# Hybrid diffusion layer on one core: twelve dense blocks beside the state scan instead of eight, merge-gate blocks ahead of attention

## The chip, the cores and the metric

The kernel runs on one core of a Trainium2 chip. The core has five engines with a queue each: TensorE (PE in the profile, with weight loads as PEld), VectorE (DVE), ScalarE (ACT), GpSimd (POOL) and SyncE (SP), which issues the DMAs here. An engine takes its instructions in the order of its queue; semaphores make it wait for others. The metric is the device time of one execution in microseconds.

## What is computed

Two layers (DEPTH = 2) over 128 context and 1024 latent tokens, 1152 together, D_MODEL = 1024, three branches 512 wide. Cut to what matters:

```python
def mixer_layer(x, cvec, lw, ctx_kv, ssm_h0, rope):
    ...
    h = rmsnorm(x, norm_g) * (1.0 + scale) + shift
    a_in, a_gate, f_in, f_gate, q, k, v, c_gate = jnp.split(h @ w_in, SPLITS, axis=-1)
    ya, finals = s5_mixer(a_in, ...)          # state scan, forward and backward
    za = jax.nn.gelu(ya) @ glu_w
    ya = za[..., :BRANCH_W] * jax.nn.sigmoid(za[..., BRANCH_W:])
    yf = fourier_mix(f_in) @ fnet_w
    ...
    yc = blocked_attention(q, k, v)           # 8 heads, 2 key heads, over 1152 keys
    branches = jnp.stack([ya * jax.nn.silu(a_gate), yf * jax.nn.silu(f_gate),
                          yc * jax.nn.silu(c_gate)], axis=2)
    proj = jnp.einsum('bsnw,nwd->bsnd', branches, w_branch)
    g = jax.nn.sigmoid(h @ merge_w + merge_b).reshape(b, s, N_BRANCH, D_MODEL)
    merged = jnp.sum(g * proj, axis=2)
    return x + gate * (merged @ w_out), k, v, finals
```

## The kernel before

Every large product is cut into dense blocks: 128 output columns, three token tiles j of 384, and K in pieces of 128 (eight for products of h, four for those of a branch). A float32 operand is split into a high and a low part; each K piece takes three matmuls (high by high, high by low, low by high) of 128x384 into a PSUM tile pd (two buffers). `dense` (line 269) yields after every four K pieces, so a **unit** is 12 matmuls; a block of K = 1024 has six units, one of K = 512 three. For every 512 rows of weights, SP loads wst, ACT copies the high part to whi and POOL subtracts to get wlo; loads run three units ahead, splits one. After its last matmul a tile is evacuated: store blocks by ACT (Silu or copy) to a tile jo (three buffers) and to DRAM, gate blocks by ACT (tanh), proj blocks by DVE (jo<-th,pd or jo<-jt,pd, then for the second and third branch jo<-jo,jt with the partial sum).

`layer` (line 1290) puts all blocks of a layer in one list and takes them from it by number. `drive` merges generators: each has a rate, and the one whose virtual time is least goes next. What it emits is then ordered for each engine by the scheduler of the language, which places an instruction when its own estimate of times lets it start; so an instruction can stand elsewhere in an engine's queue than in the program. Stages of layer 0, in order:

- a_in and f_in blocks, with set-up of the state space, then `state_gen`, which makes the inputs of the scan.
- **Scan**: `scan_gen` (line 706): 128 steps of four dependent DVE instructions on H (A in the profile), 128x128 for the first 16 steps, 128x64 after them. At step 24 it calls `finals` (line 728): ACT copies the state of step 16 to ss_fin, PE transposes it, ACT copies it out (qk_sq), SP stores it. Beside it run eight dense blocks (a and f gates). The q, k, v generator has started and has split its weights (qkW).
- **q, k, v**: per 128 tokens 24 matmuls into a PSUM tile pt (two buffers); ACT sums squares (qk_j), DVE and POOL make qk_ss and qk_rs, DVE reads pt into qk_xn. Two dense blocks beside it.
- **Output of the scan** (`ssm_out_gen`) with six blocks, **GLU** with nine, **Fourier** (`fnet_gen`) with three.
- **Attention** (`attn_gen`): 64 steps, a head and 128 queries each. A step is: six matmuls into pa (scores, one buffer), DVE's maximum at_mx, ACT's exponential at_P, DVE's reciprocal and scaling of at_P; then the nine transposes of the step before, split by ACT and DVE into at_PT; every second step 18 matmuls P·V into pv, ACT at_t, DVE at_Y. `PACE` says how many units of dense work follow an even and an odd step: (1, 2).
- zc load, gates and projections of the third branch, output product, then the same for layer 1.

In attention, `merges` takes the dense list: one gate block, the four Fourier output blocks, one gate block beside the split load of branch a (`zload_gen`: tiles jt and jo, ACT A<-jt and A<-jo, POOL the rest), eight proj blocks, one gate block beside the load of branch b, then gates and projections of branch b in turn.

Of the kernel before, what the change touches and what calls it, by code (L numbers as in the profile page):

```python
# [17 lines left out]
D = 1024  # L18
# [3 lines left out]
NT = SP + SL  # L22
# [62 lines left out]

PACE = (1, 2)
HELD = 2
# [14 lines left out]
class Program:  # L102
# [71 lines left out]

    # ---------------------------------------------------------------- constants
    def setup(self):
# [57 lines left out]

    # ---------------------------------------------------------------- weights
    def wload(self, ap):
# [56 lines left out]

    # ---------------------------------------------------------------- adaLN
    def ada_alloc(self, l):
# [91 lines left out]

    # ---------------------------------------------------------------- token-major x to feature-major
    def load_x(self, t0, t1):
# [27 lines left out]

    # ---------------------------------------------------------------- norm
    def ssq_alloc(self):
# [105 lines left out]

    # ---------------------------------------------------------------- S5
    def ssm_setup_gen(self, l):
# [178 lines left out]
    def scan_gen(self, l):  # L706
        S, H = self.S, self.H
        for k in range(128):
            n = 2 if k < 16 else 1
            if n == 2:  # L710
                cur, nxt = H[:, :, :, k:k + 18:17], H[:, :, :, k + 1:k + 19:17]
                AR = S["AR"][:, :, :, None].to_broadcast([128, 2, 32, 2])
                AI = S["AI"][:, :, :, None].to_broadcast([128, 2, 32, 2])
            else:
                cur, nxt = H[:, :, :, k + 17:k + 18], H[:, :, :, k + 18:k + 19]
                AR, AI = S["AR"][:, :, :, None], S["AI"][:, :, :, None]
            t1 = self.sb("ss_s1", [128, 2, 32, 2], bufs=2, pool=self.gp)
            t2 = self.sb("ss_s2", [128, 2, 32, 2], bufs=2, pool=self.gp)
            t1, t2 = t1[:, :, :, :n], t2[:, :, :, :n]
            self.tt(t1, AR, cur, OP.mult)  # L720
            self.tt(t2, AI, cur[:, ::-1], OP.mult)
            self.tt(t1, t1, nxt, OP.add)
            self.tt(nxt, t1, t2, OP.add)
            if k == 24:
                self.finals(l)
            yield 800

    def finals(self, l):
# [89 lines left out]

    # ---------------------------------------------------------------- q, k, v
    def qkv_tables(self, l):  # L820
# [168 lines left out]

    # ---------------------------------------------------------------- FNet  # L990
    def fnet_tables(self):
# [81 lines left out]

    # ---------------------------------------------------------------- attention
    def softmax(self, src, n, P):
# [159 lines left out]

    # ---------------------------------------------------------------- the layers
    def zload_gen(self, z_d, zf, dve=True, held=0):
# [52 lines left out]
    def layer(self, l, cs):  # L1290
# [15 lines left out]
        zt = {}  # L1306
# [49 lines left out]
        def proj_block(n, b, th, key):  # L1356
            def ev(j, ps):
                t = self.jt(rows(th["d"], b, j)) if "d" in th else th.pop(j)
                pt = self.jt(rows(t_d[n - 1], b, j)) if n > 0 else None
# [12 lines left out]
        tha = {"d": dt_("tha", (D, NT))}  # L1372
        thb = {"d": dt_("thb", (256, NT))}

# [36 lines left out]
        self.dense_add(self.store_blocks(w_in, C_CG, 4, sg_d[2], AF.Silu))  # L1411
        self.dense_add([gate_block(0, b, tha) for b in range(5)])
        self.dense_add(glu_blocks())
        self.dense_add([gate_block(0, b, tha) for b in range(5, 8)])
        self.dense_add([gate_block(1, 0, thb)])
        self.dense_add(fw_blocks())
        self.dense_add([gate_block(1, 1, thb)])
        self.dense_add([proj_block(0, b, tha, "a") for b in range(8)])
        for b in range(2, 8):
            th = {}  # L1420
            self.dense_add([gate_block(1, b, th), proj_block(1, b, th, "b")])
            if b < 4:
                self.dense_add([proj_block(1, b - 2, thb, "b")])
        self.dense_add([gate_block(2, b, thc[b]) for b in range(8)])
# [5 lines left out]
        with self.spool:  # L1430
# [11 lines left out]
            with self.pool("qp", l):  # L1442
                with self.pool("gp", l, "q"):
                    self.qkt = self.qkv_tables(l)
                    def qkv():
                        yield from self.qkv_gen(l, qs_d, k_d, v_d, (0,))
                        yield from self.qkv_gen(l, qs_d, k_d, v_d, (1,))
                    q = qkv()
                    self.run_some(q, 8)
                    drive((self.scan_gen(l), 103), (self.dense(8), 106))  # L1450
                    drive((q, 78), (self.dense(2), 21))
# [6 lines left out]
        with self.pool("gp", l, "f"):  # L1458
            self.fnet_tables()
            zt["f"] = self.sb("A1", [128, 2, 4, NT], R)  # L1460
            run(self.dense(1))
            drive((self.dense(2), 32), (self.fnet_gen(l, f_d, zt["f"]), 48))
        with self.pool("gp", l, "a"):
            def merges():
# [5 lines left out]
                yield from self.beside(self.zload_gen(zb_d, zt["b"], False, 2), self.dense(1), 1)  # L1470
                yield from self.dense(13)
            m = merges()
# [122 lines left out]
```

## Time and profile before

| what | value |
|---|---|
| device time of three runs | 2791.06, 2797.77, 2800.18 us; median 2797.77 |
| span of the profiled execution, first to last instruction | 2790.2 us |
| median of the runs less that span | 7.6 us |
| busy: PE, DVE, ACT, POOL | 94%, 65%, 42%, 24% |
| mean granted TensorE clock | 0.975 of 2.4 GHz |

The device time of the profiled execution itself is not listed apart from its span. Stages of layer 0 by the timeline: scan 190 to 353 us, q, k, v to 462, output of the scan to 518, GLU to 645, Fourier to 735, attention to 1158. Times on the timeline are microseconds from the start of the span; in brackets stands the time that the engine sat idle before an instruction, and what ended it.

### The profile page before, as it was taken

To read this page: it belongs to the slowest core of one execution; us is meant where nothing else is said; L and a number is where in the kernel's file an instruction comes from. 1 tells how busy PE (TensorE), PEld (TensorE's weight loads), DVE (VectorE), ACT (ScalarE), POOL (GpSimd) and SP (SyncE) were. 2 spreads that over 40 slices of the span, in tenths; PEclk is the share of its full clock that TensorE was granted. 3 is DMA by queue.
4 is the path that set the end of the run, shared out by engine and by line. 5 is a ranking of instruction groups with operands and counts; after the bars stand their busy time and mean duration, and the time that the engine had idled before them with its cause. 6 is when DMAs were issued, how large, how long until landed. Compare 5 with 4: busy or idle time off the path is not lost.

```text
span 2790.2 us, 44375 instructions
## 1 busy us (share of the span) xinstructions
PE 2615.0 (94%) x16092; PEld 2516.5 (90%) x16092; DVE 1807.5 (65%) x3933; ACT 1158.2 (42%) x2688; POOL 679.0 (24%) x521
## 2 busy tenths in 40 slices
PE   7998698999999999999999895989999999999998
PEld 3998698998999999999989895979989999999997
DVE  6559956764577777766573797575666777771343
ACT  5461154432455555423345322543235454553244
POOL 3231123222321210132343220322233020102223
PEclk9999899999999999999999997999999999999999
DMA  6632134474444422444542321356626444213244
GB/s 223 174 101 88 49 111 120 138 213 159 159 144 148 140 87 74 136 125 118 170 143 83 99 92 37 112 147 171 220 96 214 133 125 139 80 47 94 82 121 145
DMA packets 449627, 352.68 MB, mean 126 GB/s; under 512 B 71800, under 2 KB 421632, under 8 KB 449408
## 3 DMA queue, kind: packets, MB, share of 16 engines
q1 hardware_dynamic: 448112, 345.59, 40.5%
q0 software_dynamic: 1296, 4.26, 0.5%
q8 instruction: 127, 2.08, 0.3%
q14 instruction: 92, 0.75, 0.1%
HBM read 236.44 MB, written 113.31 MB: 125 GB/s over the span
## 4 chain that ended last, share of the span: by engine, by line
PE 65%; DVE 20%; issue 5%; DMA 5%; ACT 3%; POOL 1%; SPq 0%; DVEq 0%; POOLq 0%; ACTq 0%
PE pd L168 41%; DVE ss_s L145 7%; PE pa L168 7%; PE pv L168 6%; PE pt L168 6%; PE pt L173 4%; DVE A L145 3%; PE pv L173 2%; DVE xr L149 1%; DMA aw<-in_ada_w_dram 1%; DVE hl L149 1%; DVE jo L149 1%; DMA tha<-jo 1%; DVE jo L145 1%; ACT A L142 1%
## 5 line engine op out<-in xcount | busy, mean ns | idle before, releaser
L168 PE MATMUL pd<-hh,whi 128*128 128x384 f32 x2496 | 859.4, 344 | 25.6 <-ACT jo L142 20.9
L168 PE MATMUL pd<-hh,wlo 128*128 128x384 f32 x2496 | 844.2, 338 | 3.1 <-POOL wlo L145 3.1
L168 PE MATMUL pd<-hl,whi 128*128 128x384 f32 x2496 | 843.1, 338 | 1.4 <-DVE hl L149 1.4
L145 POOL TENSOR_TENSOR wlo<-wst,whi 128x512 fp32r<-128x512 f32 x312 | 436.8, 1402 | 1541.4 <-ACT whi L142 1451.7
L168 PEld LDWEIGHTS pd<-hh,whi 128*128 128x128 f32 x2496 | 472.2, 189 | 36.5 <-ACT jo L142 23.5
L168 PEld LDWEIGHTS pd<-hh,wlo 128*128 128x128 f32 x2496 | 472.5, 189 | 7.7 <-POOL wlo L145 5.8
L168 PEld LDWEIGHTS pd<-hl,whi 128*128 128x128 f32 x2496 | 473.2, 190 | 5.3 <-DVE hl L149 2.3
L168 PE MATMUL pd<-A,whi 128*128 128x384 f32 x1728 | 449.1, 340 | 8.3 <-ACT jo L142 4.5
L168 PEld LDWEIGHTS pd<-A,whi 128*128 128x128 f32 x1728 | 307.5, 189 | 12.3 <-DVE jo L149 6.2
L142 ACT ACTIVATE whi<-wst 128x512 fp32r<-128x512 f32 x312 | 195.8, 630 | 245.8 <-PE pd L168 167.9
L168 PE MATMUL pd<-A,wlo 128*128 128x384 f32 x864 | 290.0, 336 | 0.0
L168 PE MATMUL pt<-qkW,hh 128*128 128x384 f32 x576 | 154.4, 350 | 59.3 <-DVE qk_xn L145 59.3
L1079 DVE TENSOR_REDUCE at_mx<-pa 128x1 f32<-128x1152 f32 x128 | 173.4, 1355 | 54.6 <-PE pa L168 54.2
L142 ACT ACTIVATE at_PT<-pt 128x384 fp32r<-128x384 f32 (+1 forms) x260 | 113.9, 490 | 188.5 <-PE pt L173 188.3
L142 ACT ACTIVATE at_P<-pa,at_mx 128x1152 f32<-128x1152 f32 x128 | 158.3, 1236 | 18.2 <-DVE at_mx L1079 17.7
L168 PEld LDWEIGHTS pd<-A,wlo 128*128 128x128 f32 x864 | 162.8, 188 | 0.1
L168 PEld LDWEIGHTS pt<-qkW,hh 128*128 128x128 f32 x576 | 107.5, 196 | 60.0 <-DVE qk_xn L145 60.0
L168 PE MATMUL pa<-at_K,at_Q 128*128 128x384 f32 x768 | 160.4, 338 | 1.1 <-DMA at_K<-kd 1.0
L168 PE MATMUL pv<-at_PT,at_V 128*128 128x256 f32 x1152 | 149.7, 284 | 0.2
L168 PEld LDWEIGHTS pv<-at_PT,at_V 128*128 128x128 f32 x1152 | 142.7, 190 | 4.6 <-DVE at_PT L145 0.8
L168 PEld LDWEIGHTS pa<-at_K,at_Q 128*128 128x128 f32 x768 | 131.5, 188 | 4.9 <-DMA at_K<-kd 2.1
L145 DVE TENSOR_TENSOR at_PT<-pt,at_PT 128x384 fp32r<-128x384 f32 (+1 forms) x260 | 132.2, 549 | 2.3 <-ACT at_PT L142 2.2
(295 smaller groups left out, 3715.4 us busy)
## 6 DMA issues: line engine op xcount, KB each, us to landing
aw<-in_ada_w_dram SPq DMA_DIRECT2D x48, 512.0 KB, 4.3
wst<-in_merge_w_dram SPq DMA_DIRECT2D x96, 256.0 KB, 3.0
wst<-in_w_in_dram SPq DMA_DIRECT2D x80, 256.0 KB, 2.9
td<-jo SPq DMA_DIRECT2D x96, 192.0 KB, 2.7
jt<-td SPq DMA_DIRECT2D x96, 192.0 KB, 2.7
wst<-in_w_out_dram SPq DMA_DIRECT2D x64, 256.0 KB, 2.7
sgd<-jo SPq DMA_DIRECT2D x72, 192.0 KB, 1.9
jt<-sgd SPq DMA_DIRECT2D x64, 192.0 KB, 3.3
```

What stands on the lines that cost most here:

```text
L142: return self.nc.scalar.activation(out, in_, func, **kw)
L145: return (e or self.nc.vector).tensor_tensor(out=out, in0=a, in1=b, op=op)
L149: return (e or self.nc.vector).scalar_tensor_tensor(out, a, s, b, op0=op0, op1=op1, **kw)
L168: return self.nc.tensor.matmul(out, w, x, start=first, stop=last, **kw)
L173: return self.nc.tensor.transpose(out, in_, i[:n, :n])
L1079: nc.vector.tensor_reduce(out=mx[:, 0:1], in_=src, axis=AX.XY if m3 else AX.X, op=OP.max, negate=True)
```

## The change

The list of blocks is put in another order, and the numbers that the stages take are changed with it: the scan gets twelve blocks (a, f and c gates) in place of eight, q, k, v and the scan's output get gate 0 blocks in place of c gates, GLU starts with a gate 1 block, Fourier gets four gate 1 blocks in place of three gate 0 blocks, and attention three gate 1 blocks in place of eight. `PACE` goes from (1, 2) to (1, 1), so attention's units fall from 108 to 78. All eight gate 1 blocks keep their tanh in DRAM (thb), and the projection loads it back to a tile th; before, two did and six kept it on chip. `finals` is called after the scan's last step.

```diff
-PACE = (1, 2)
+PACE = (1, 1)
...
-            if k == 24:
-                self.finals(l)
             yield 800
+        self.finals(l)
...
         def proj_block(n, b, th, key):
             def ev(j, ps):
-                t = self.jt(rows(th["d"], b, j)) if "d" in th else th.pop(j)
+                if n == 1:
+                    t = th_tile()
+                    self.dma(t, rows(th["d"], b, j))
+                else:
+                    t = self.jt(rows(th["d"], b, j)) if "d" in th else th.pop(j)
...
-        thb = {"d": dt_("thb", (256, NT))}
+        thb = {"d": dt_("thb", (D, NT))}
...
-        self.dense_add([gate_block(0, b, tha) for b in range(5)])
+        self.dense_add([gate_block(0, b, tha) for b in range(8)])
+        self.dense_add([gate_block(1, 0, thb)])
         self.dense_add(glu_blocks())
-        self.dense_add([gate_block(0, b, tha) for b in range(5, 8)])
-        self.dense_add([gate_block(1, 0, thb)])
+        self.dense_add([gate_block(1, b, thb) for b in range(1, 6)])
         self.dense_add(fw_blocks())
-        self.dense_add([gate_block(1, 1, thb)])
+        self.dense_add([gate_block(1, 6, thb)])
         self.dense_add([proj_block(0, b, tha, "a") for b in range(8)])
-        for b in range(2, 8):
...
+        self.dense_add([gate_block(1, 7, thb)])
+        self.dense_add([proj_block(1, b, thb, "b") for b in range(8)])
...
-                    drive((self.scan_gen(l), 103), (self.dense(8), 106))
+                    drive((self.scan_gen(l), 103), (self.dense(12), 140))
...
-            drive((self.dense(2), 32), (self.fnet_gen(l, f_d, zt["f"]), 48))
+            drive((self.dense(3), 48), (self.fnet_gen(l, f_d, zt["f"]), 48))
...
                 yield from self.beside(self.zload_gen(zb_d, zt["b"], False, 2), self.dense(1), 1)
-                yield from self.dense(13)
+                yield from self.dense(8)
```

What it moves in the engines' queues is shown at three places. The first is ACT early in the scan of layer 0, before the change (jo are the evacuations of the dense tiles, ss_fin the copy of the final state, qk_sq its way out):

```order
L142 ACT_TABLE_LOAD
L142 ACTIVATE jo<-pd 128x384 x2
L142 ACTIVATE whi<-wst 128x512
L142 ACTIVATE ss_fin<-A_1197 128x64
L142 ACTIVATE whi<-wst 128x512
L142 ACTIVATE jo<-pd 128x384 x3
L142 ACTIVATE whi<-wst 128x512
L142 ACTIVATE qk_sq<-pv 32x128 x2
```

And ACT at the same place after it:

```order
L142 ACT_TABLE_LOAD
L142 ACTIVATE jo<-pd 128x384 x2
L142 ACTIVATE whi<-wst 128x512
L142 ACTIVATE ss_fin<-A_1197 128x64
L142 ACTIVATE whi<-wst 128x512
L142 ACTIVATE jo<-pd 128x384 x3
L142 ACTIVATE whi<-wst 128x512 x2
```

ss_fin keeps its place behind two jo and a whi; qk_sq has moved to the end of the stage.

The second is POOL through the scan of layer 0, as a piece of the difference (wlo is the low part of a weight tile, qk_rs the scale of the q, k, v rows):

```order
 L145 TENSOR_TENSOR wlo<-wst,whi 128x512 x2
 L145 TENSOR_TENSOR qkW_1994<-jt,qkW_1993 128x384
-L145 TENSOR_TENSOR wlo<-wst,whi 128x512 x16
+L145 TENSOR_TENSOR wlo<-wst,whi 128x512 x24
 L145 TENSOR_TENSOR qk_rs<-qk_ss,half 128x4 x7
 L145 TENSOR_TENSOR wlo<-wst,whi 128x512
```

Eight more weight splits stand ahead of the first qk_rs.

The third is DVE in attention of layer 0, where projections of branch b run beside it. Before the change, one step without P·V and the beginning of the next:

```order
L1079 TENSOR_REDUCE at_mx<-pa 128x1
L145 TENSOR_TENSOR at_PT_10973<-pt,at_PT_10972 128x3x128 x2
L145 TENSOR_TENSOR at_PT_10973<-pv,at_PT_10972 128x3x128
L1082 RECIPROCAL at_mx<-at_mx 128x1
L1083 TENSOR_SCALAR at_P<-at_P,at_mx 128x1152
L149 SCALAR_TENSOR_TENSOR jo<-th,pd 128x384
L145 TENSOR_TENSOR jo<-jo,jt 128x384
L1079 TENSOR_REDUCE at_mx<-pa 128x1
```

After it, such a step and the next:

```order
L1078 TENSOR_REDUCE at_mx<-pa 128x1
L145 TENSOR_TENSOR at_PT_12013<-pt,at_PT_12012 128x3x128 x2
L145 TENSOR_TENSOR at_PT_12013<-pv,at_PT_12012 128x3x128
L1081 RECIPROCAL at_mx<-at_mx 128x1
L149 SCALAR_TENSOR_TENSOR jo<-th,pd 128x384
L1082 TENSOR_SCALAR at_P<-at_P,at_mx 128x1152
L1078 TENSOR_REDUCE at_mx<-pa 128x1
L145 TENSOR_TENSOR at_PT_12013<-pt,at_PT_12012 128x3x128 x2
L145 TENSOR_TENSOR at_PT_12013<-pv,at_PT_12012 128x3x128
L145 TENSOR_TENSOR jo<-jo,jt 128x384
L1081 RECIPROCAL at_mx<-at_mx 128x1
```

The first half of the projection's evacuation, which reads pd, has moved ahead of the scaling of at_P. On PE, the step without P·V has 11 or 12 dense matmuls between its transposes and the next scores, where 24 stood.

## Rows read from the trace of the kernel before

**Rows 1.** Page, part 1: busy us, share and count of each engine.
```profile
PE 2615.0 (94%) x16092; PEld 2516.5 (90%) x16092; DVE 1807.5 (65%) x3933; ACT 1158.2 (42%) x2688; POOL 679.0 (24%) x521
```

**Rows 2.** Waits of PE: who waited for whom; us in total, times, longest.
```profile
PE pt L168 <- DVE qk_xn L145: 59.3, 2, 29.7
PE pd L168 <- ACT jo L142: 25.4, 8, 7.8
```

**Rows 3.** Windows: us, busy PE, PEld, DVE, ACT, POOL (instructions), clock, DMA share, GB/s.
```profile
190.00:353.20 163.20, 124.92 (x704) 123.29 (x702) 153.46 (x539) 30.52 (x68) 30.84 (x22) 0.89 0.24 76
735.00:1158.00 423.00, 422.17 (x2805) 414.41 (x2803) 310.12 (x523) 221.37 (x456) 73.47 (x60) 1.00 0.39 123
```

**Rows 4.** Timeline of PE where the scan ends: start, us, instruction, [idle before].
```profile
310.69 0.52 PE L168 MATMUL pt<-qkW,hh 128*128 128x384 f32 x2
...
323.17 0.34 PE L168 MATMUL pd<-hh,wlo 128*128 128x384 f32 x1
353.17 1.01 PE L168 MATMUL pt<-qkW,hh 128*128 128x384 f32 x2 [29.67 <-DVE qk_xn L145]
...
1711.37 1.01 PE L168 MATMUL pt<-qkW,hh 128*128 128x384 f32 x2 [29.64 <-DVE qk_xn L145]
```

**Rows 5.** Windows around the two stalls of layer 0's scan; the clock is third from the end.
```profile
230.00:310.00 80.00, 80.00 (x464) 79.65 (x463) 75.41 (x268) 17.31 (x34) 16.45 (x13) 1.00 0.27 87
...
353.20:359.10 5.90, 5.90 (x19) 5.90 (x20) 2.41 (x9) 2.31 (x12) 1.01 (x1) 0.50 0.23 69
...
224.90:229.30 4.40, 4.35 (x14) 4.36 (x15) 4.19 (x15) 0.37 (x1) 0.96 (x1) 0.50 0.46 149
```

**Rows 6.** Timeline of DVE at the scan's last instruction.
```profile
351.26 0.28 DVE L145 TENSOR_TENSOR A<-ss_s,ss_s 128x64 f32<-128x64 f32 x1
```

**Rows 7.** Timeline of ACT and PE at ss_fin.
```profile
223.68 0.32 ACT L142 ACTIVATE ss_fin<-A 128x64 f32<-128x64 f32 x1 [12.25 <-DVE A L145]
...
224.95 0.69 PE L168 MATMUL pd<-hh,whi 128*128 128x384 f32 x1 [7.83 <-ACT jo L142]
```

**Rows 8.** Timeline of POOL and DVE in the scan, at a weight split.
```profile
309.39 1.28 POOL L145 TENSOR_TENSOR wlo<-wst,whi 128x512 fp32r<-128x512 f32 x1 [9.12 <-ACT whi L142]
...
309.13 0.28 DVE L145 TENSOR_TENSOR A<-ss_s,ss_s 128x64 f32<-128x64 f32 x1
309.44 1.36 DVE L145 TENSOR_TENSOR ss_s<-ss_AR,A 128x64 f32<-128x64 f32 x1
```

**Rows 9.** Windows of two attention steps each, projections of branch b and a.
```profile
1000.83:1013.35 12.52, 12.52 (x86) 12.36 (x85) 9.42 (x17) 6.51 (x13) 1.30 (x1) 1.00 0.42 135
...
830.29:842.81 12.52, 12.52 (x86) 12.35 (x85) 9.36 (x17) 5.92 (x12) 1.30 (x1) 1.00 0.39 116
```

**Rows 10.** Timeline of PE in an attention step: scores and the first dense matmul.
```profile
1005.80 1.20 PE L168 MATMUL pa<-at_K,at_Q 128*128 128x384 f32 x6
...
1007.75 0.42 PE L168 MATMUL pd<-hh,whi 128*128 128x384 f32 x1
```

**Rows 11.** Timeline of DVE and ACT in the same step.
```profile
1007.04 1.36 DVE L1079 TENSOR_REDUCE at_mx<-pa 128x1 f32<-128x1152 f32 x1 [0.82 <-PE pa L168]
...
1010.05 0.82 DVE L1083 TENSOR_SCALAR at_P<-at_P,at_mx 128x1152 f32<-128x1152 f32 x1
...
1008.50 1.24 ACT L142 ACTIVATE at_P<-pa,at_mx 128x1152 f32<-128x1152 f32 x1
```

**Rows 12.** The tile at_P on DVE: ns min/median/max, first and last start.
```profile
L1083 DVE TENSOR_SCALAR at_P<-at_P,at_mx x128: 809/821/1502, 755.5 to 2510.3; 128x1152 f32<-128x1152 f32 x128
```

**Rows 13.** Timeline of PE where the second key block is loaded.
```profile
955.96 0.80 PE L168 MATMUL pa<-at_K,at_Q 128*128 128x384 f32 x3 [0.15 <-DMA at_K<-kd]
```

**Rows 14.** Timeline of ACT where branch b is loaded and split.
```profile
910.05 0.53 ACT L142 ACTIVATE A<-jo 128x384 fp32r<-128x384 f32 x1 [0.53 <-DMA jo<-zbd]
```

**Rows 15.** A short wait of PE in q, k, v, and the window after it.
```profile
400.00 0.62 PE L173 MATMUL pa<-identr,qk_kk 128*128 128x128 f32 x3 [1.83 <-ACT qk_qo L142]
...
400.00:403.40 3.40, 3.40 (x14) 3.40 (x15) 3.37 (x9) 1.54 (x6) 1.46 (x2) 0.51 0.92 271
```

More of the change, by code (lines that the diff above doesn't have):

```diff
@@ L1411, in layer @@
         self.dense_add(self.store_blocks(w_in, C_CG, 4, sg_d[2], AF.Silu))
-        self.dense_add([gate_block(0, b, tha) for b in range(5)])
+        self.dense_add([gate_block(0, b, tha) for b in range(8)])
+        self.dense_add([gate_block(1, 0, thb)])
         self.dense_add(glu_blocks())
-        self.dense_add([gate_block(0, b, tha) for b in range(5, 8)])
-        self.dense_add([gate_block(1, 0, thb)])
+        self.dense_add([gate_block(1, b, thb) for b in range(1, 6)])
         self.dense_add(fw_blocks())
-        self.dense_add([gate_block(1, 1, thb)])
+        self.dense_add([gate_block(1, 6, thb)])
         self.dense_add([proj_block(0, b, tha, "a") for b in range(8)])
-        for b in range(2, 8):
[L1420 to L1423, printed above, removed]
+        self.dense_add([gate_block(1, 7, thb)])
+        self.dense_add([proj_block(1, b, thb, "b") for b in range(8)])
         self.dense_add([gate_block(2, b, thc[b]) for b in range(8)])
```

## Prediction

> **What bounds the kernel now.** I read the page's busy shares first, then who waited for whom on TensorE (PE), then busy time by stage, then the timeline where PE stood still. PE is busy 94% of the span [rows 1], so a change pays only where it takes away PE idle time, or moves PE work into it. PE's waits have two big entries, both from one place in each of the two layers: 59.3 us in two waits on VectorE's (DVE's) qk_xn and 25.4 us in eight waits on ScalarE's (ACT's) jo [rows 2]. The stage table agrees: in the state-scan stage (190 to 353.2 us) PE works 124.9 of 163.2 us, while in attention (735 to 1158 us) it works 422.2 of 423 us [rows 3]. The reader is to see that before the change attention has no PE time to give away and the scan stage has 38 us of it.
>
> The timeline shows the hole. PE finishes the eight dense blocks, starts the q/k/v product at 310.69 us and stops at 323.5; it resumes at 353.17 after 29.67 us, and in layer 1 at 1711.37 after 29.64 us [rows 4]. What it waits for stands behind the scan in DVE's queue: the scan's last instruction runs at 351.26 us [rows 6]. After the hole PE's clock is at its lower level: from 353.2 to 359.1 the granted clock is 0.50, that is 1.2 GHz, against 1.00 (2.4 GHz) in the run before [rows 5]. That costs half of 5.9 us, 2.95 us more.
>
> **The change part by part.**
>
> *Four more blocks beside the scan.* A dense matmul takes 80.00 us / 464 = 0.1724 us at full clock [rows 5]; a unit (four k, three matmuls each) is 12 of them, 2.07 us. A block of eight k is six units, so four more blocks are 24 units, 288 x 0.1724 = 49.7 us. PE therefore ends the dense blocks at 310.7 + 49.7 = 360.4 us, and has its 12.8 us of q/k/v work (310.7 to 323.5) before it needs qk_xn, at 373.2 us. Does the scan end by then? Each dense unit of this kind brings a weight split on GpSimd (wlo on POOL), and the DVE instruction of the scan that meets it takes 1.36 us in place of 0.28 [rows 8]; sixteen such splits become 24 in the stage (the order of POOL shows x16 against x24). So the scan ends 8 x 1.08 = 8.6 us later, at 351.5 + 8.6 = 360.1 us, and qk_xn follows within 2 us. PE needs it 11 us after that. The hole closes and with it the slow-clock stretch: 29.67 + 2.95 = 32.6 us a layer, **65.2 us** in all. If the cover were gone (a scan 11 us longer than reckoned), each further microsecond would be one of PE's again.
>
> *The final states (finals) after the scan instead of at step 24.* One would expect 7.83 us a layer here: at 223.68 us ACT takes up ss_fin after 12.25 us of waiting for the scan's step 16, jo behind it frees no PSUM, and PE stands 7.83 us and then runs 4.4 us at half clock [rows 5, 7]. But the order shows ss_fin at the same place of ACT's queue as before, behind the same two jo and one whi, because the instruction depends only on that step and the scheduler places it by its own estimate. So the stall stays; I cost the edit at **0**. Behind ss_fin wait, as before, whi and three jo, and PE for these. What does move is the transpose of ss_fin on PE and its copy, to the end of the stage, where two small matmuls cost nothing.
>
> *The cg, gate and proj blocks in other places.* Their matmuls are the same in number, so PE's work does not change. Gates take the places that cg leaves beside q/k/v and the scan's output, and the Fourier stage gets one block more (6 units, 12.4 us of PE); all are evacuated by ACT as before. Six activation-table loads a layer vanish from ACT's order, since Silu no longer alternates with Gelu; ACT is not what PE waits for there: 0.
>
> *tanh of gate 1 through DRAM.* 18 more stores and 18 more loads a layer on SP. The loads go to th, which has three buffers, so each waits for the multiply three tiles back, and weight loads are queued behind it on SP. Those run three units (6 us and more) ahead; 0, at most 1 us a layer.
>
> *Attention with 78 units of dense work instead of 108.* This is the other side of the account. PE must now finish two steps (two score blocks, one P·V) with two units instead of three: 12.52 - 2.07 = 10.45 us [rows 9]. No engine's sum forbids it: DVE is busy 9.42 us and ACT 6.51 us of two steps with two gate/proj evacuations of the costliest kind [rows 9], 90% and 62%. The chain inside a step is what can. Scores start at 1005.80 us, DVE's maximum at 1007.04, ACT's exponential at 1008.50, and it takes 1.24 us [rows 10, 11]; only then is the one PSUM buffer pa free for the next scores: 1.24 + 1.46 + 1.24 = 3.94 us. In the step without P·V, PE covered that with 24 matmuls; it now has the scores and transposes, 1.95 us (1005.80 to 1007.75 [rows 10]), and 11 matmuls, 1.9 us: 3.85 us, and waits about 0.1 us. Further, DVE's order now has the evacuation jo<-th,pd ahead of the scaling of at_P. Scaling ended 3.83 us after the maximum began (1010.05 + 0.82 less 1007.04 [rows 11]); with 0.55 us more it ends 1.24 + 3.83 + 0.55 = 5.62 us after the scores began, while PE wants to transpose after the next scores and three matmuls, at 3.94 + 1.05 + 0.52 = 5.5 us: another 0.1 to 0.2 us. In the step with P·V there are 2 us to spare. So I take 0.3 us for each pair of steps; 26 regular pairs a layer: 8 us.
>
> Two odd places come to it. When the second key block is loaded (single buffer), PE waited 0.15 us with two units of cover [rows 13]; with one unit less it can wait up to 2.07 us more; I take 2 us. In the two stretches where branch tiles are split on ACT (A<-jo, 0.53 us each, twelve a stretch, now and then behind a DMA [rows 14]), exponentials stand behind these; I take 2 us each. Sum 8 + 2 + 4 = **14 us a layer, 28 us**. Its lower end is 3 us (the 0.1 us alone). The upper end is where POOL's splits meet the scaling of at_P, which takes 0.82 us at the median and 1.50 at most [rows 12]: 26 splits x 0.68 = 18 us more, 32 us a layer. I take 14, since with a split in each pair DVE's sum in rows 9 shows hardly any stretching.
>
> The Trainium skill (SBUF — State Buffer, Who interferes with whom) says that a DVE instruction that uses the shared port pair waits for the whole GpSimd instruction. If each of 26 splits cost its full 1.28 us there, attention would lose 47 us a layer and the kernel would be at about 2827 us; row 12's maximum of 1.50 us speaks for half of that.
>
> **The sum.** 2790.2 us of span - 65.2 + 28 = 2753 us. The median of the runs, 2797.8, is 7.6 us above this span, so I carry the difference of -37 us to it: **2761 us**.
>
> **The rivals.**
>
> *Attention gives everything back and PE waits nowhere* (3 us a layer): 2797.8 - 65.2 + 6 = 2739 us. For it: PE's idle there is nil now. Against: 3.85 us of work against a chain of 3.94.
>
> *The ss_fin stall goes too*, as the edit says: 7.83 + 2.2 us a layer less, 2761 - 20 = 2741 us. Against: the same place in ACT's queue.
>
> *DVE's in-order queue makes PE wait in every pair; slower than before.* If the evacuation ahead of the scaling waits for a dense unit that PE ends only after the next scores and three matmuls (5.5 us, then 0.2 drain and 0.55), scaling ends at about 7.1 instead of 5.6 us and the transposes with it: 1.5 us a pair, 26 x 1.5 + 6 = 45 us a layer, 2797.8 - 65.2 + 90 = 2823 us. It decides from 32.6 / 26 = 1.25 us a pair. For it: the order has the evacuation first. Against: the unit read there is mostly the one that PE ended before those scores.
>
> *The gain is eaten, no change*: the upper end of attention's cost, 32 us a layer, 2797 us.
>
> *PE's short waits bring its clock down in attention.* After 1.83 us of idle the profile shows 3.4 us at 0.51 [rows 15], a loss of 1.7 us. One such drop in every third pair is 9 x 1.7 = 15 us a layer, 2761 + 30 = 2791 us. Waits of 0.3 us speak against it. The Trainium skill (TensorE: Matmul & The Clock Gate, A second HAM failure mode: psum-queue depth-cycling) tells of such a kernel, whose short idles between matmul groups kept switching the clock; by that rule this case is the likelier one, and attention's clock of 1.00 [rows 9] shows only that it has no idles yet.
>
> **How the numbers follow.** Forecast (2743 to 2780) 0.62; attention free of waits 0.09; ss_fin too 0.07; gain eaten 0.07; clock 0.03; slower 0.12. A measurement of this kernel can tell about 0.3% (8 us) from no change. Faster 0.62 + 0.09 + 0.07 = 0.78, same 0.07 + 0.03 = 0.10, slower 0.12. The range leaves out the slower case and most of the eaten one above, and takes in 2739 below less the runs' scatter: 2736 to 2790 us.
>
> **What will show it.** PE's wait on qk_xn (59.3 us) must be gone or under 5 us, with the scan's end near 360 us and the clock at 1.00 after it. PE's 7.8 us wait behind ss_fin must still be there, once a layer. In attention a pair of steps must take 10.6 to 10.9 us, and PE's waits on pa, at_P or at_PT must sum to 15 to 30 us over both layers. A pair above 11.7 us would make the prediction wrong in sign; a scan that ends after 373 us would make it wrong in its first step.

## The result and the profile after

The changed kernel takes 2752.96 us (median of 2750.34 to 2756.89), the kernel before 2797.47 us: ratio 0.9846, 95% interval 0.9833 to 0.986, or 44.5 us less. The forecast was 2761 us. The two profiled executions lie closer together, 2790.2 and 2750.3 us of span, 39.9 us less against the 37 us of the sum. The other 4.6 us lie in the first runs of the kernel before: the median of four is 2797.47 us, and 31 later ones, in three groups, have medians of 2791 to 2793 us.

The page's first part, of the changed kernel (busy time, share of the span, instructions):

```profile
span 2750.3 us, 44553 instructions
PE 2627.0 (96%) x16092; PEld 2509.0 (91%) x16092; DVE 1826.6 (66%) x3933; ACT 1143.5 (42%) x2676; POOL 683.4 (25%) x521
```

PE's waits after the change (line waited for, total us, times, longest):

```profile
PE pd L168 <- ACT jo L142: 25.1, 8, 7.8
...
PE pt L173 <- DVE at_P L1082: 8.4, 13, 1.0
...
PE pa L168 <- DVE ss_Hg L805: 6.4, 5, 2.3
...
PE pa L168 <- ACT at_P L142: 5.8, 7, 1.3
```

The 59.3 us on qk_xn of [rows 2] have left the list. The waits on jo are what they were, 25.1 against 25.4 us. New are waits of attention's transposes (pt) and scores (pa) on at_P, 14.2 us together.

Windows of the changed kernel, in the columns of [rows 3]: the old scan stage, the stretch that ran at half clock before, layer 0's attention, and two pairs of attention steps.

```profile
190.00:353.20 163.20, 154.65 (x874) 153.70 (x873) 154.85 (x517) 36.98 (x72) 38.11 (x27) 0.97 0.30 96
353.20:359.10 5.90, 5.90 (x36) 5.90 (x35) 4.65 (x20) 0.85 (x2) 0.00 (x0) 1.00 0.18 67
768.10:1144.70 376.60, 367.00 (x2442) 349.34 (x2441) 311.06 (x524) 203.83 (x428) 57.94 (x48) 1.00 0.44 136
1083.54:1094.37 10.83, 10.83 (x75) 10.48 (x74) 10.72 (x18) 5.82 (x12) 1.29 (x1) 1.00 0.50 135
1100.99:1112.77 11.78, 11.05 (x75) 10.45 (x74) 10.68 (x18) 5.81 (x12) 1.28 (x1) 1.00 0.40 123
```

In the 163.2 us of [rows 3] PE now works 154.65 us in place of 124.92, and the next 5.9 us hold 36 matmuls at a clock of 1.00, where [rows 5] had 19 at 0.50. Attention, in turn, is no longer full: 367.0 of 376.6 us.

To follow the time further I give each stage a **loss**: for each matmul, the time to the start of the next less the median of that time for the same product in the kernel before, summed. Idle time, half clock and waits too short for the profile's list all count. Both kernels issue the same 16092 matmuls, so the differences of the losses must add up to that of the spans.

| loss, us, layer 0 / layer 1 | before | after | difference |
|---|---|---|---|
| scan | 12.1 / 12.2 | 12.3 / 12.2 | +0.2 / 0 |
| q, k, v (with the hole) | 41.4 / 41.9 | 9.8 / 10.2 | -31.6 / -31.7 |
| output of the scan | 21.1 / 21.2 | 18.4 / 17.8 | -2.7 / -3.4 |
| GLU and Fourier | 20.3 / 16.6 | 20.0 / 16.7 | -0.3 / +0.1 |
| attention | 5.6 / 6.5 | 22.5 / 21.7 | +16.9 / +15.2 |
| what follows | 23.3 / 8.9 | 24.4 / 5.2 | +1.1 / -3.7 |

Gain 63.3, price 32.1, and some 9 us of small change elsewhere: -40.

### The profile page after: what moved, and what is told of

It reads as the page before. It is cut to its first block, busy times and chain, and to the rows that moved or that the text cites. A ratio compares the mean times of both kernels' runs of the same rounds, so it can differ in the third digit from the quotient of the medians.

```text
span 2750.3 us, 44553 instructions
## 1 busy us (share of the span) xinstructions
PE 2627.0 (96%) x16092; PEld 2509.0 (91%) x16092; DVE 1826.6 (66%) x3933; ACT 1143.5 (42%) x2676; POOL 683.4 (25%) x521
## 5 line engine op out<-in xcount | busy, mean ns | idle before, releaser
L168 PE MATMUL pd<-hh,whi 128*128 128x384 f32 x2496 | 857.1, 344 | 24.0 <-ACT jo L142 20.1
L168 PE MATMUL pd<-A,whi 128*128 128x384 f32 x1728 | 458.2, 342 | 8.2 <-ACT jo L142 4.9
L168 PEld LDWEIGHTS pd<-A,whi 128*128 128x128 f32 x1728 | 311.2, 189 | 11.7 <-ACT jo L142 5.6
L168 PE MATMUL pa<-at_K,at_Q 128*128 128x384 f32 x768 | 167.2, 347 | 8.6 <-ACT at_P L142 5.8
L142 ACT ACTIVATE at_P<-pa,at_mx 128x1152 f32<-128x1152 f32 x128 | 158.1, 1235 | 20.7 <-DVE at_mx L1078 19.4
L168 PEld LDWEIGHTS pd<-A,wlo 128*128 128x128 f32 x864 | 163.2, 189 | 0.1
L142 ACT ACTIVATE jo<-pd 128x384 f32<-128x384 f32 x120 | 58.0, 485 | 198.1 <-PE pd L168 96.5
```

The lines of the kernel that those rows point to most:

```text
L142: return self.nc.scalar.activation(out, in_, func, **kw)
L168: return self.nc.tensor.matmul(out, w, x, start=first, stop=last, **kw)
```

## The experiments

In the runs below the kernel before, taken anew beside them, has medians of 2791 to 2793 us. Differences between kernels are therefore taken from the ratios to the kernel before, times 2797 us; one thousandth is 2.8 us. The changed kernel itself ran beside the first runs alone, so its distance to the kernels below is known to some 4 us: taken from the medians as they stand, the distances come out 2 to 4 us larger or smaller than given here. My theory is the prediction's: the scan's hole is the gain, attention's lost cover the price, and the moved finals does nothing. The main rivals are that finals has a part in the gain, and that the price comes from something other than the pace.

### The edit of finals by itself

```diff
-            if k == 24:
-                self.finals(l)
             yield 800
+        self.finals(l)
```

> The kernel before with one edit of the change alone: finals is called after the scan's last step. My theory: ss_fin keeps its place in ACT's queue, so ACT still waits about 12 us for the scan's step 16 and PE still stands 7.8 us once a layer; no change, 2797 us, within 8 us. The rival (the edit removes the stall, as its text says): 7.8 us of idle and 2.2 us of half clock go in each layer, about 2777 us.

Measured: 2791.82 us against 2792.26, ratio 0.9999 (0.9989 to 1.0008). ACT and PE of this kernel, on the timeline (in brackets the idle time before):

```profile
223.47 0.32 ACT L142 ACTIVATE ss_fin<-A 128x64 f32<-128x64 f32 x1 [12.20 <-DVE A L145]
...
224.74 0.69 PE L168 MATMUL pd<-hh,whi 128*128 128x384 f32 x1 [7.79 <-ACT jo L142]
```

The call moved in the program, and the instruction did not move in ACT's queue, as the order had it. The edit is worth nothing, in either kernel: the changed one has the same two lines with 12.25 and 7.84.

### The stall itself taken away

The changed kernel, with the copy made by DVE, whose queue holds the step that it waits for:

```diff
+            if k == 24:
+                fin = self.sb("ss_fin", [128, 2, 32], pool=self.gp)
+                self.nc.vector.tensor_copy(fin, H[:, :, :, 16])
             yield 800
-        self.finals(l)
+        self.finals(l, fin)
...
-        fin = self.sb("ss_fin", [128, 2, 32], pool=self.gp)
-        self.act(fin, H[:, :, :, 16])
```

> The changed kernel with the copy of the final state to ss_fin made by DVE, at step 24, in place of ACT; its transposes stay after the scan. My theory: the wait in ACT's queue was all of the stall, so 7.8 us of idle and 2.2 us of half clock go in each layer, and since the twelve blocks then end at about 351 us and PE needs qk_xn at 364, with the scan ending at 358, no new wait takes their place: 2753 - 20 = 2733 us. A rival: the time comes back as a wait for qk_xn; then half or less is left, 2743 us or more.

Measured: 2730.21 us, ratio 0.9778 (0.9763 to 0.9792), 0.0068 or 19 us below the changed kernel. PE's waits, and then windows of the scan and of what follows it:

```profile
PE pd L168 <- ACT jo L142: 8.1, 6, 2.1
```

```profile
189.50:349.50 160.00, 159.36 (x918) 158.64 (x916) 152.02 (x500) 37.90 (x73) 40.30 (x28) 1.00 0.32 101
349.50:376.00 26.50, 26.50 (x155) 26.16 (x154) 17.79 (x70) 10.42 (x50) 5.46 (x6) 1.00 0.22 65
```

The waits on jo fall by 17 us, the scan's loss from 12.3 to about 1.6 us in layer 0. PE reaches q, k, v at 349.5 us and does not wait there, though the scan now ends at 360.1 us: the twelve blocks reach just far enough for this too. So this stall is a price of its own, 10 us a layer, which the change meant to take and left.

### The pace of attention by itself

```diff
-PACE = (1, 2)
+PACE = (1, 1)
```

> The kernel before with PACE (1, 1) alone: attention gets 78 or so units of dense work in place of 108, and what is left of the list runs behind it. The scan keeps eight blocks and its hole. My theory: this is the price that the change pays in attention, by itself. Between the two traces attention's loss (its time over what its matmuls take back to back) rises by 17 us in layer 0 and 15 us in layer 1, so 2797 + 32 = 2829 us. A rival: part of that loss comes from the other order of the blocks or from the th loads, and the pace alone costs under 15 us, below 2812 us.

Measured: 2822.45 us, ratio 1.0104 (1.0087 to 1.0121), +29 us. PE's waits:

```profile
PE pt L168 <- DVE qk_xn L145: 59.7, 2, 30.3
...
PE pa L168 <- ACT at_P L142: 6.5, 7, 1.6
PE pt L173 <- DVE at_P L1083: 5.7, 8, 0.8
```

The hole is where it was, and attention's waits on at_P are those of the changed kernel; its loss there is 22.5 and 20.8 us, again as in the changed kernel. The rival that blames the th loads or the order of the blocks falls: one number of the change makes the whole price, 31 of 32 us by the loss.

### Another number of blocks beside the scan

The changed kernel with ten blocks there and four beside q, k, v:

```diff
-                    drive((self.scan_gen(l), 103), (self.dense(12), 140))
-                    drive((q, 78), (self.dense(2), 21))
+                    drive((self.scan_gen(l), 103), (self.dense(10), 123))
+                    drive((q, 78), (self.dense(4), 42))
```

> The changed kernel with ten dense blocks beside the scan in place of twelve, the two taken away run beside q, k, v. My theory, the prediction's sum at another size: PE needs qk_xn 24.8 us earlier, at 348.8 us; the scan ends 4 splits x 1.08 us earlier, near 354, and PE resumes 1.6 us behind it: a hole of about 7 us and 2 us of half clock in each layer, so 18 us more than the changed kernel, 2771 us. A rival (each of the four blocks brings a quarter of the gain): 16 us a layer, 2785 us. If weight splits did not stretch the scan, it would end at 358 here too and the hole would be 11 us, 2779 us.

Measured: 2776.7 us, ratio 0.9942 (0.9924 to 0.996), 27 us above the changed kernel. PE on the timeline where the scan ends, and then a window behind it:

```profile
357.47 1.01 PE L168 MATMUL pt<-qkW,hh 128*128 128x384 f32 x2 [7.27 <-DVE qk_xn L145]
```

```profile
357.50:361.50 4.00, 4.00 (x13) 4.00 (x14) 2.13 (x9) 1.93 (x11) 1.01 (x1) 0.50 0.30 92
```

The hole is of the size that the sum gives (7.27 us, in layer 1 6.57), and half clock follows it for some 4 us; the loss of q, k, v rises by 10.1 and 9.7 us, 20 in all. The scan ends at 355.8 us with 24 stretched instructions, in the changed kernel at 358.2 with 26, so the reading in which splits do not stretch it (358 us, a hole of 11) falls too. The whole time rose by 7 us more. In the trace, 4 of them lie in layer 0's stage after attention, whose loss lies between 23.3 and 28.6 us in kernels that have the same code there; I count them as scatter, which is argued and not shown. That a quarter of the gain goes with each block is what the total alone would suggest (27 of 63 us for two of four blocks); the hole of 7 us shows that it is not so.

### What in attention PE waits for

The changed kernel without POOL's splits in attention, where `inatt` is set; the low part of the weights is missing there:

```diff
         self.act(hi[:, :nk], st[:, :nk])
+        if self.inatt:
+            return hi, hi
...
         self.tt(lo[:, :nk], st[:, :nk], hi[:, :nk].bitcast(F), OP.subtract, e=self.nc.gpsimd)
```

> The changed kernel without POOL's weight splits in attention: the low part of the weights is left out there, and the high part is used twice, so that PE's matmuls are the same in number. My theory: the 13 waits on DVE's at_P in the changed kernel (8.4 us) stand where a split meets the scaling of at_P and go, the waits of the scores on ACT's at_P stay: 8 to 12 us less than the changed kernel, about 2743 us, ratio 0.981 to before. A rival (each of the 26 splits a layer costs its whole 1.28 us): far more than that, 20 us and up. Another (the splits cost nothing that PE sees): 2753 us.

Measured: 2743.43 us, ratio 0.9819 (0.9801 to 0.9838), 7.6 us below the changed kernel, though the intervals of the two touch. The trace is plainer. The scaling of at_P on DVE (ns min/median/max) in the changed kernel and, in the second fence, PE's waits in this one:

```profile
L1082 DVE TENSOR_SCALAR at_P<-at_P,at_mx x128: 808/820/1924, 782.4 to 2475.1; 128x1152 f32<-128x1152 f32 x128
```

```profile
PE pa L169 <- ACT at_P L143: 2.9, 3, 1.3
PE pt L174 <- DVE at_P L1085: 2.1, 3, 1.0
```

In the changed kernel 20 of the 128 scalings take over 1 us, eighteen of them 1.88 to 1.92; in the kernel before it was two, of 1.50 [rows 12]; here it is six, of which four meet the splits that are left at attention's end, two in each layer. With them go the waits of the transposes, 8.4 to 2.1 us, and attention's loss falls from 22.5 to 16.0 and from 21.7 to 16.2 us. One such meeting in the changed kernel, DVE, POOL and PE:

```profile
1103.92 0.55 DVE L149 SCALAR_TENSOR_TENSOR jo<-th,pd 128x384 f32<-128x384 f32 x1
1104.39 1.89 DVE L1082 TENSOR_SCALAR at_P<-at_P,at_mx 128x1152 f32<-128x1152 f32 x1
...
1104.37 1.28 POOL L145 TENSOR_TENSOR wlo<-wst,whi 128x512 fp32r<-128x512 f32 x1 [15.64 <-ACT whi L142]
...
1106.42 0.85 PE L173 MATMUL pt<-ident,at_P 128*128 128x128 f32 x6 [0.73 <-DVE at_P L1082]
```

The split starts 0.02 us before the scaling, which then takes 1.89 us in place of 0.82; the transposes wait. That is the pair of 11.78 us above, and the meeting lies in the step without P·V. The pair of 10.83 us holds a meeting too, in its step with P·V, and is no longer than the pair that begins one step later, which has none:

```profile
1087.46 1.89 DVE L1082 TENSOR_SCALAR at_P<-at_P,at_mx 128x1152 f32<-128x1152 f32 x1
```

```profile
1090.16:1100.99 10.83, 10.83 (x75) 10.48 (x74) 9.73 (x17) 5.29 (x11) 0.00 (x0) 1.00 0.56 160
```

DVE works 9.73 us of a pair without a meeting and 10.72 of one with it, so a meeting leaves it almost no slack.

A shorter chain, in the changed kernel:

```diff
-        nc.vector.tensor_reduce(out=mx[:, 0:1], in_=src, axis=AX.XY if m3 else AX.X, op=OP.max, negate=True)
+        nc.vector.tensor_reduce(out=mx[:, 0:1], in_=src[:, 0] if m3 else src, axis=AX.X, op=OP.max, negate=True)
...
-        self.act(dst, src, AF.Exp, bias=mx[:, 0:1], accum=mx[:, 1:2])
+        self.act(dst, src, AF.Exp, bias=mx[:, 0:1], scale=0.25, accum=mx[:, 1:2])
```

> The changed kernel with a shorter chain in attention: the maximum is taken over the first 384 of 1152 scores, and the exponential is of a quarter of the scores; the rest of the softmax's work is left as it is. DVE's maximum falls from 1.36 to about 0.55 us, so the chain scores, maximum, exponential is 3.1 us in place of 3.94. My theory: the chain is what attention's short steps wait for, so the waits of scores and transposes on at_P go nearly all and attention's loss falls from 22 to 10 us or less a layer: 24 us less, about 2729 us, ratio 0.976 to before. A rival (the loss is the irregular places and the sum of DVE's work): 10 us less or fewer, 2743 us and above.

Measured: 2733.93 us, ratio 0.9786 (0.9769 to 0.9803), 17 us below the changed kernel: nearer to the theory's 24 than to the rival's 10, and neither. Every wait on at_P is gone from PE's list. Layer 0's attention:

```profile
766.30:1129.90 363.60, 360.00 (x2416) 345.39 (x2415) 259.51 (x523) 209.71 (x428) 58.09 (x48) 1.00 0.44 136
```

The loss falls to 13.8 and 12.4 us, not to 10, and it is made of other pieces now: in layer 0 5.3 us stand where P·V begins behind at_PT, 0.2 us at each of 27, and 6 us in gaps of 0.08 us between matmuls into pd, which the kernel before has too (2.95 us). A pair takes 10.64 us at the median. With less work in the chain the scores are free and the next link, at_PT, is left; what the last 0.2 us a pair wait for was not tried apart.

The run does not part the chain from two other things that changed with it. DVE has 51.6 us less to do in this stretch (259.51 against 311.06 us), and the meetings have gone too, though POOL's splits have not. The scaling stands right behind the reciprocal again in 124 of 128 cases, and none is long:

```profile
L1082 DVE TENSOR_SCALAR at_P<-at_P,at_mx x128: 809/820/1028, 780.2 to 2451.6; 128x1152 f32<-128x1152 f32 x128
```

Of the 9 us that a layer gains here, some 6 are thus those of the run without splits. What is left for the chain and for DVE's smaller sum is about 3 us a layer, and which of the two it is was not shown. The median pair, which a meeting does not touch, tells the same: 10.8 us in the changed kernel and without splits, 10.64 here.

### The gain without the price

The kernel before, with twelve blocks beside the scan, where the four extra ones come from the stage after attention: four gate 2 blocks go ahead, their tanh to DRAM, and attention keeps its 108 units.

```diff
-        self.dense_add([gate_block(0, b, tha) for b in range(5)])
+        self.dense_add([gate_block(0, b, tha) for b in range(8)])
+        self.dense_add([gate_block(2, 0, thg)])
         self.dense_add(glu_blocks())
-        self.dense_add([gate_block(0, b, tha) for b in range(5, 8)])
+        self.dense_add([gate_block(2, b, thg) for b in range(1, 4)])
...
-        self.dense_add([gate_block(2, b, thc[b]) for b in range(8)])
+        self.dense_add([gate_block(2, b, thc[b]) for b in range(4, 8)])
...
-                    drive((self.scan_gen(l), 103), (self.dense(8), 106))
+                    drive((self.scan_gen(l), 103), (self.dense(12), 140))
...
```

The lines left out behind this let the next layer's modulation work run on beside the projections of branch c, since only four gate blocks are left there.

> The kernel before with twelve blocks beside the scan, where the four extra ones come from the stage after attention (four of the eight gate 2 blocks, their tanh stored to DRAM and loaded by the projection of branch c) and not from attention, which keeps its 108 units and PACE (1, 2). My theory: gain and price of the change are two separate things; this has the gain of the closed hole, 32 us a layer, and no price: 2797 - 63 = 2734 us. A rival: the stage after attention cannot give up 24 units, because the next layer's modulation work (aw loads, DVE) runs beside it and becomes late: 2745 to 2760 us.

Measured: 2739.73 us, ratio 0.9809 (0.9794 to 0.9824), -53 us: 10 less than the theory's 63, and the rival's mechanism at a lower price. Attention's loss is 6.7 and 5.5 us, as before; q, k, v lose 11.0 and 9.6, as after the change. But the last stage of layer 0 loses 36.7 us in place of 23.3 (layer 1, which has no next layer to prepare, 11.1 in place of 8.9). PE there:

```profile
1235.56 1.01 PE L168 MATMUL pd<-A,whi 128*128 128x384 f32 x2 [4.98 <-DVE jo L149]
```

With DVE's copy of the final state in addition:

> The four extra blocks from the stage after attention, as in the run before of that kind, and in addition the copy of the final state made by DVE. My theory: the two gains add up, since they are two waits one after the other and the twelve blocks still reach past the scan's end: ratio 0.9809 less 0.007, 0.974, near 2720 us. A rival: with the stall gone PE reaches q, k, v ten us earlier and waits there: 0.978 and above.

Measured: 2716.06 us, ratio 0.9726 (0.9705 to 0.9747), 77 us less than the kernel before and 34 less than the changed one. The two gains add up; this is the fastest kernel that ran. Its windows behind attention of layer 0, and those of the kernel before:

```profile
1164.80:1254.30 89.50, 84.21 (x490) 80.33 (x489) 82.64 (x131) 27.41 (x51) 26.46 (x13) 1.00 0.63 199
```

```profile
1160.50:1250.00 89.50, 87.66 (x526) 85.51 (x525) 60.32 (x92) 25.53 (x47) 27.80 (x13) 1.00 0.53 167
```

DVE is busy 82.64 of 89.5 us there, against 60.32: with fewer gate blocks the modulation work reaches into the projections of branch c, whose evacuations are DVE's too (21.5 us of them in this window, none in that of the kernel before). Beginning it earlier was the attempt to bring time back; against the run just shown:

```diff
             def last():
-                yield from self.dense(3)
+                yield from self.dense(4)
...
-            run(self.dense(1))
             if l + 1 < DEPTH:
-                drive((last(), 41), (self.ada_side_gen(l + 1, self.gp, (2, 0, 3, 1)), 10))
+                drive((last(), 41), (self.ada_side_gen(l + 1, self.gp, (2, 0, 3, 1)), 14))
```

> The last version (four gate 2 blocks ahead, final state copied by DVE), with the next layer's modulation work begun one block earlier and at a higher rate, so that it lies beside the gate blocks, which ACT evacuates, and not beside the projections of branch c, which DVE evacuates with three instructions a tile. In that version and the one without DVE's copy, layer 0's last stage loses 9 to 13 us more than in the kernel before, in waits for jo from DVE. My theory: it is DVE's queue; with the modulation out of the way 8 us come back, ratio 0.9726 less 0.003, near 0.970. A rival: its 0.5 MB loads at the higher rate make the weight loads late, and PE waits for wlo: 0.973 or above.

Measured: 2727.02 us, ratio 0.9768 (0.9749 to 0.9787): slower than without it. PE's waits on DVE's jo rose from 13.5 to 20.7 us, the longest of them 7.2 us at 1230.7 us:

```profile
PE pd L168 <- DVE jo L149: 20.7, 14, 7.2
```

The ratio is the rival's, the mechanism is not: PE's waits on wlo are 1.8 us, against 3.4 without this edit, so the loads were not what it waited for. The engine was named rightly and the remedy was wrong. Ahead of the evacuation that ends the longest wait, twelve modulation instructions (aacc) stand in a row in DVE's queue:

```profile
1222.12 8.03 DVE L149 SCALAR_TENSOR_TENSOR aacc<-aw,silc,aacc 128x512 f32<-128x512 f32 x12
1230.07 0.55 DVE L149 SCALAR_TENSOR_TENSOR jo<-thc,pd 128x384 f32<-128x384 f32 x1
```

Whether DVE has too much work in this stretch as a whole, or only too much of it in a row, was not tried apart.

## Why the prediction was right, and where its terms were off

**The scan's hole: right.** Forecast -65.2 us, found -63.3 in the stage's loss. The last instruction of the scan and the first qk_xn in the changed kernel:

```profile
357.88 0.28 DVE L145 TENSOR_TENSOR A<-ss_s,ss_s 128x64 f32<-128x64 f32 x1
...
370.30 0.42 DVE L145 TENSOR_TENSOR qk_xn<-pt,qk_rs 128x256 f32<-128x256 f32 x1 [1.12 <-POOL qk_rs L145]
```

The scan ends at 358.2 us, forecast 360.1: six more splits fell into it, not eight, 26 of its instructions were stretched in place of 20, to 1.34 us on average. PE came to q, k, v at 360.8 us (forecast 360.4), after the scan's end. The run with ten blocks had the sum's hole too.

**finals at nothing: right**, by a run of its own (0.9999), and the stall that it leaves by another (19 us, priced 20).

**Attention: right in place and pace, and in part by luck in size.** Forecast 14 us a layer, found 16.9 and 15.2. A pair of regular steps takes 10.8 us at the median; the forecast was 10.6 to 10.9. PE's listed waits on at_P are 14.2 us, just under the 15 to 30 that I named, since half of the loss is in waits too short for that list. The term that was mis-sized is the meeting of POOL's splits with the scaling of at_P. I priced one at 0.68 us from the longest row of the kernel before and then took it for rare, since DVE's sum showed no stretching. That row was misread. The scaling of 1.50 us met no weight split but the shorter split of a branch tile, which had begun 0.13 us before it; POOL and DVE in the kernel before:

```profile
777.82 1.01 POOL L145 TENSOR_TENSOR A<-jt,A 128x384 fp32r<-128x384 f32 x1 [11.83 <-ACT A L142]
...
777.95 1.50 DVE L1083 TENSOR_SCALAR at_P<-at_P,at_mx 128x1152 f32<-128x1152 f32 x1
```

No weight split makes a scaling longer there. In the changed kernel one costs 1.07 us (1.89 less 0.82) nine times a layer, and 0.74 us a tenth time, though attention has 24 splits a layer in place of 36 (the forecast counted 26). The pace alone, in its own run, brings it 12 times in both layers together.

The order of DVE tells where it comes from. In the kernel before, the scaling stands right behind the reciprocal in 120 of 128 cases, and most of the splits near it begin 0.3 to 0.7 us after it. In the changed kernel, and in the run of the pace alone, every scaling of 1.87 us and more stands right behind an evacuation, which delays it until the split begins, to within 0.03 us. That the evacuation put ahead is the reason is read from these traces; no run moved it alone.

In both layers the scalings take 20.5 us more of DVE's time than at their median, against 1.3 before. What saved the sum is that PE sees only part of this, since a meeting in a step with P·V can cost nothing (10.83 us), and that the terms for the odd places were taken large enough.

Here the rule of the Trainium skill (SBUF — State Buffer, Who interferes with whom) is that of a GpSimd instruction and a DVE instruction that uses the shared port pair, whichever issues first keeps the pair for its whole length and the other blocks. The prediction took up one half of it, and the trace agrees with both: a scaling is delayed by 1.07 us behind a split of 1.28, and a split that begins 0.42 us after a scaling takes 1.54 us and leaves the scaling at 0.82. That each of 26 splits costs so much, which would have made 2827 us, did not hold; the trace of the run without splits puts the whole price at 6 us a layer.

**Slower, and clock drops: fell.** Of the 29 pairs of layer 0 from the fourth step on, five are above 11.7 us, a length that would have made the change slower had every pair taken it, and one of these, at the key load, is longer than 12.3 us. The clock is 1.00 over attention. So the rule on short idles between matmuls that switch the clock (the Trainium skill, TensorE: Matmul & The Clock Gate, A second HAM failure mode: psum-queue depth-cycling) finds no case here: waits of up to 1.3 us left the clock alone.

**Off the sum: 9 us.** I costed six activation-table loads a layer at 0, and the output of the scan, where gates took the place of the c gates, loses 3 us less in each layer. The same 18 us or so of loss stand there in the other kernels with that order (17.6 to 20.1), and 19.5 to 23.9 in the kernel before and the two runs that keep its order. The ranges overlap, and that the table loads are the cause was not tried apart; other blocks stand there as well. The span came out within 3 us of the sum because these 9 us cancel attention's 4 us more and the hole's 2 us less: that much is luck.

## What to carry to other kernels

An engine that waits in one stage and is full in another is fed by moving work between them, but the work moved was also cover for a chain where it stood: price that chain (here 3.94 us a step, against 3.85 of work) and look for a third place that has neither chain nor hole, which here was worth 10 us more, though it had a price of its own in DVE's queue. Moving a call in a program that a scheduler orders may move nothing; see where the instruction stands in its queue, and put a copy on the engine that makes its input. When one engine's instruction lengthens another's, count how often the two start together after the change, not before it.

## What was not expected of the hardware

A POOL split of 128x512 (1.28 us) that starts with the scaling, a DVE instruction of 128x1152, makes it 1.89 us long in place of 0.82, and eighteen of the 128 have this length within 0.04 us. In the scan, an instruction of 128x64 takes 1.36 us in place of 0.28 [rows 8]: the delay is 1.07 and 1.08 us, for one that is short and one that is long. The 26 stretched ones in the changed kernel's scan take 1.11 to 1.51 us. The delay depends on who starts first. Two scalings that begin 0.36 us into a split take 1.56 us, and a split that begins while a scaling runs is itself the longer one, up to 1.85 us; POOL and DVE in the changed kernel:

```profile
838.55 1.54 POOL L145 TENSOR_TENSOR wlo<-wst,whi 128x512 fp32r<-128x512 f32 x1 [2.04 <-ACT whi L142]
...
838.13 0.82 DVE L1082 TENSOR_SCALAR at_P<-at_P,at_mx 128x1152 f32<-128x1152 f32 x1
```

The maximum, which reads pa in PSUM, is never longer: its 128 instructions take 1.34 to 1.36 us, beside a split or not.
